# Hybrid decoder trunk: the first two weight groups of each feed-forward stage side by side, token parts split two at once

## The chip, the cores and the metric

The kernel runs on one core of one Trainium2 chip. The metric is the device time of the whole program in microseconds (us); lower is better.

## The reference

512 tokens of width 1024 pass through two layers. Each layer adds half a SwiGLU feed-forward (width 2816), then a mixer, then half of a second feed-forward; each of the three takes a root-mean-square norm of the running sum `h`. All in float32:

```
for layer in range(DEPTH):                       # DEPTH = 2
    h = h + 0.5 * _swiglu(_rmsnorm(h, norm_ffn1[layer]), ffn1_wg[layer], ffn1_wu[layer], ffn1_wd[layer])
    hn = _rmsnorm(h, norm_mix[layer])
    if layer % 2 == 0:
        h = h + _attn_conv_mixer(hn, ...)        # windowed attention | causal convolution, one output projection
    else:
        h = h + _recurrent_mixer(hn, ...)        # gated linear recurrence, output projection
    h = h + 0.5 * _swiglu(_rmsnorm(h, norm_ffn2[layer]), ffn2_wg[layer], ffn2_wu[layer], ffn2_wd[layer])
return _rmsnorm(h, norm_final)

def _swiglu(x, wg, wu, wd):
    return (jax.nn.silu(x @ wg) * (x @ wu)) @ wd
```

So there are four feed-forward stages, one even and one odd mixer, and a final norm.

## The kernel before, in words

**Products.** Tensors lie with the model width on the 128 partitions and the 512 tokens along the free axis. A float32 product is made of three matmuls of a rounded high half and a low rest: high by high, high by low, low by high. ScalarE (ACT) makes the high half (`hi`) by a copy to fp32r, VectorE (DVE) the low half (`lo`) by a subtraction. That holds for the weights (`raw` to `hi` and `lo`, tiles of 128 x 1024 or 128 x 768) and for the tokens (`split`, tiles named `t`).

**Seven products for eight.** The four feed-forward stages take the token axis and the inner axis in halves and use the seven-product form of a 2 x 2 block product. The products are called 1 to 7. Each wants one weight form, summed from four raw blocks, and one token part. `FORMS` says how a weight form is made: `q` holds block 0 (form 1); block 2, loaded into `r`, is added by DVE (form 7); block 3 and later block 1 are added to `q` by accumulating DMAs on GpSimd's (POOL's) queue (forms 6 and 3); block 3 is added to `r` the same way (form 5); forms 2 and 4 are plain loads on SyncE's (SP's) queue. The forms of one `q` are thus a chain. `Quarters` holds the token side: `make` builds one part (for 5, 7, 6 and 4 a difference first), then splits it into one tile, high half left, low half right.

**A stage.** The 22 chunks of the inner width are paired into 11 groups, in three rounds (`ROUNDS`) of 4, 4 and 3. Group 0 is multiplied the plain way (`two_by_chunk`, `project`) out of the unnormalized tokens and scaled afterwards by the norm factor `r`; its matmuls run while `r` is found (`inv_root`: a sum over partitions, then twelve small DVE operations). When `r` is there, the 28 token parts of the normed input (`xq`, four chunks by seven) are made, in the order 1, 2, 7, 5 and 6, 3, 4. The other groups take the seven products, 24 matmuls of 256 columns each. After each round two down groups (`downs`) take the round's results back to the model width, with 24 matmuls a product, 18 in the last round, and their products are added to `h` (`add_to`). `BANK` says which PSUM bank a product uses: 1, 6, 5 and 3 follow each other in `u`, 7 and 4 in `v`, 2 has `w`; a later product of a bank waits until the earlier sum has been read. `sequence` fixes the order of products: that of a group interleaves with the one before it.

**The order of instructions.** All operations are first recorded by `Plan.add` and then ordered for each engine by a list scheduler (`Plan.schedule`) with modelled costs; each operation has a due time, the matmul time recorded so far plus `plan.late`. An operation with a positive `late` is low: it may take a new `t` tile only when seven are free (`RESERVE`). Pools of numbered tiles limit how far things run ahead: `T_SLOTS` tiles `t` of 2 KB a partition, `RAWS` raw weights, `PARTS` high and as many low weight halves, of 4 KB each. `take` has weights recorded twelve units ahead (`AHEAD`), due 25 us early (`EARLY_PREP`), and the `hi` copies keep the order of the units. Since every instruction is emitted in `Plan.emit`, all of them carry line 426 in the profile; tiles tell them apart.

Of the kernel before, what the change touches and what calls it, by code (L numbers as in the profile page):

```python
# [64 lines left out]
T_SLOTS = 70  # L65
RAWS = 7
PARTS = 4
# [4 lines left out]
START_PREP = 9000.0  # L72
EARLY_LN = -40000.0
# [108 lines left out]
class Plan:  # L182
# [59 lines left out]
    def add(self, alts, late=None, after=None):  # L242
# [3 lines left out]
        for meth, a, k in alts[0][1]:  # L246
            for i, v in enumerate(a):
                if isinstance(v, _View):
                    (writes if i == 0 else reads).append(v.vt)
            for key, v in k.items():  # L250
                if isinstance(v, _View):
                    (writes if key in ("out", "accum_out") else reads).append(v.vt)
        op.alts = []
        op.table = None
        for eng, calls in alts:
            cs = [self.cost(eng, *c) for c in calls]
            op.alts.append((eng, sum(c for c, _ in cs), any(l for _, l in cs), calls))
# [12 lines left out]
        for t in reads:  # L270
            assert t.writers, t.name
            op.preds.update(t.writers[-1:])
# [157 lines left out]
def trunk(ctx, tc, A, out):  # L430
# [34 lines left out]
    class Group:  # L465


        def __init__(self, aps, chunks):
            self.aps, self.chunks = aps, chunks
            self.n = 2 * chunks * P  # L470
            self.raw, self.w, self.banks, self.open = {}, {}, {}, set()

    def sequence(groups, needs):


        out, last = [], None
        for g in groups:
            if last is None:
                out += [(g, "1", 0), (g, "2", 0), (g, "7", 0), (g, "6", 0)]
            elif needs(g, last):  # L480

                out += [(g, "1", 0), (last, "5", 0), (g, "7", 1), (last, "3", 0), (last, "4", 0)]
                out += [(g, "7", 2), (g, "6", 0), (g, "2", 0)]
            else:
                out += [(g, "1", 0), (last, "5", 0), (g, "2", 0), (g, "7", 0), (last, "3", 0), (last, "4", 0), (g, "6", 0)]
            last = g
        return out + [(last, m, 0) for m in ("5", "3", "4")]

    def ffn_units(w, l, final):
# [4 lines left out]
        for r, members in enumerate(ROUNDS):  # L494
# [4 lines left out]
            for d in DUALS[: 1 if final and r == len(ROUNDS) - 1 else 2]:  # L499
# [3 lines left out]
                order.append(downs[r, d])  # L503
        steps = sequence(order, lambda g, last: g in downs.values() and last in ffs.values())
# [64 lines left out]
    def prep_():  # L569
# [5 lines left out]
        else:  # L575
            n = src.n
            key, load, other, more = FORMS[what]
            for k, b in load.items():
# [3 lines left out]
            if other is not None:  # L582
                nc.vector.tensor_tensor(out=raw[:, :n], in0=raw[:, :n], in1=src.raw[other][:, :n], op=ALU.add)
            if more is not None:
                kw = dict(out=raw[:, :n], in_=src.aps[more], accum_op=ALU.add)
                plan.add([("SW", [("dma_start", (), kw)])])
        hi = plan.tile("hi", (P, WMAX), F32R)
# [56 lines left out]
    h = [pairs[j // 2][:, j % 2, :] for j in range(NJ)]  # L644
# [91 lines left out]
    def inv_root(parts, inv_n, eps, b0=0, nb=NB):  # L736
        pst = ps()
        for b in range(b0, b0 + nb):
# [6 lines left out]
        nc.vector.tensor_scalar(out=v[:], in0=pst[:, :nb], scalar1=inv_n, scalar2=eps, op0=ALU.mult, op1=ALU.add)  # L745
        nc.vector.tensor_scalar(out=sh[:], in0=v[:].bitcast(I32), scalar1=1, scalar2=None, op0=ALU.logical_shift_right)
        nc.vector.tensor_scalar(
            out=y[:].bitcast(I32), in0=sh[:], scalar1=-1, scalar2=0x5F3759DF, op0=ALU.mult, op1=ALU.add
        )
        for _ in range(3):  # L750
            nc.vector.tensor_tensor(out=w[:], in0=y[:], in1=y[:], op=ALU.mult)
            nc.vector.scalar_tensor_tensor(out=w[:], in0=w[:], scalar=-0.5, in1=v[:], op0=ALU.mult, op1=ALU.mult)
            nc.vector.scalar_tensor_tensor(out=y[:], in0=w[:], scalar=1.5, in1=y[:], op0=ALU.add, op1=ALU.mult)
# [38 lines left out]
    def scaled(o, r):  # L792
        t = tt()
        late, plan.late = plan.late, EARLY_EVICT
# [7 lines left out]
    class Quarters:  # L802
# [13 lines left out]
        def make(self, m):  # L816
# [9 lines left out]
            elif m == "4":  # L826
                ve.scalar_tensor_tensor(out=t[:, HI], in0=t[:, LO], in1=b[:, LO], **kw)
            src = {
# [5 lines left out]
            self.parts[m] = x[:, LO], x[:, HI]  # L834

# [26 lines left out]
    def ffn(which, gain, gain_next):  # L862
# [20 lines left out]
        for names in (("1",), ("2",), ("7",), ("5", "6"), ("3",), ("4",)):  # L883
            for j, q in enumerate(xq):
                for m in names:
                    if m == "1":
                        normed(q.a, j, LO)
                    elif m == "2":
# [614 lines left out]
```

## Time and profile before

| | |
|---|---|
| median of 3 runs | 1756.18 us (1755.38 to 1757.98) |
| profiled execution | 1756.76 us |
| its span, first to last instruction | 1755.0 us |
| mean granted clock of TensorE | 0.984 of 2.4 GHz |
| busy in the span | TensorE 1693.3, VectorE 1430.5, ScalarE 963.9, GpSimd 259.7 us |
| HBM read | 264.90 MB, 153 GB/s over the span |

The profile is of one execution. An engine's busy time is what its instructions cover; the time between is idle, and the profile names what released the instruction behind it. TensorE (PE) is near the whole span; what it doesn't cover lies in a few places, which the rows below single out. The four feed-forward stages run at about 0 to 355, 490 to 880, 880 to 1235 and 1400 to 1755 us, the even mixer between the first and the second, the odd one between the third and the fourth.

### The profile page before, as it was taken

The page shows a single profiled execution, that of the slowest core. Times are in us where ns is not written, and L with a number is a line of the kernel's source. Part 1 is how long each engine was busy: PE and PEld are TensorE (multiplying, and loading weights), DVE is VectorE, ACT ScalarE, POOL GpSimd, SP SyncE. Part 2 cuts the span into 40 slices and gives each one's busy share as a digit, 9 for nine tenths or more (in the row PEclk, how much of TensorE's full clock was granted, in tenths as well). Part 3 has the DMA queues.
Part 4 walks back from the last instruction along what each step waited for, and adds up shares of the span by engine and source line. Part 5 has one row for each costly group of instructions (what it writes and reads, how often), then busy time and mean ns, then how long its engine had stood idle before and what let it go on. Part 6 is the DMA issues. An engine that isn't in the chain of part 4 may idle for free. (4 is left out here: it accounts for less than half of the span.)

```text
span 1755.0 us, 31057 instructions
## 1 busy us (share of the span) xinstructions
PE 1693.3 (96%) x12294; PEld 1591.3 (91%) x12294; DVE 1430.5 (82%) x2382; ACT 963.9 (55%) x1611; POOL 259.7 (15%) x286
## 2 busy tenths in 40 slices
PE   8999999999899999999998999999999989999997
PEld 6899999978578899999978999999787889999997
DVE  7987877879957987877899878778788598778686
ACT  5755645554634654645556546455485366465465
POOL 0011111118502111111100111111011011111110
PEclk8999999999989999999999999999999999999999
DMA  6687777632013677777646677776332256776761
GB/s 222 147 239 192 183 179 194 151 117 89 32 68 89 146 185 188 187 176 194 153 127 158 180 182 192 179 192 153 107 120 84 84 133 169 178 197 170 198 151 49
DMA packets 78257, 269.02 MB, mean 153 GB/s; under 512 B 8688, under 2 KB 11040, under 8 KB 77984
## 3 DMA queue, kind: packets, MB, share of 16 engines
q0 software_dynamic: 27216, 96.35, 31.9%
q1 hardware_dynamic: 50896, 170.69, 26.9%
q8 instruction: 96, 1.57, 0.4%
q14 instruction: 49, 0.40, 0.1%
HBM read 264.90 MB, written 3.68 MB: 153 GB/s over the span
## 5 line engine op out<-in xcount | busy, mean ns | idle before, releaser
L426 PE MATMUL ps<-t,hi 128*128 128x256 f32 (+1 forms) x7948 | 1573.8, 298 | 29.5 <-ACT t L426 13.6
L426 PEld LDWEIGHTS ps<-t,hi 128*128 128x128 f32 x7948 | 1266.0, 190 | 85.9 <-ACT t L426 20.3
L426 PE MATMUL ps<-t,lo 128*128 128x256 f32 (+1 forms) x3974 | 1180.0, 297 | 8.4 <-DVE lo L426 8.2
L426 ACT ACTIVATE hi<-raw 128x1024 fp32r<-128x1024 f32 (+1 forms) x507 | 520.3, 1037 | 503.3 <-PE ps L426 218.5
L426 PEld LDWEIGHTS ps<-t,lo 128*128 128x128 f32 x3974 | 756.7, 190 | 33.5 <-DVE lo L426 11.2
L426 DVE TENSOR_TENSOR lo<-raw,hi 128x1024 fp32r<-128x1024 f32 (+1 forms) x498 | 590.4, 1195 | 181.7 <-ACT hi L426 179.2
L426 ACT ACTIVATE t<-t 128x256 fp32r<-128x256 f32 (+4 forms) x605 | 241.0, 428 | 199.9 <-DVE t L426 194.0
L426 DVE TENSOR_TENSOR t<-t,t 128x256 fp32r<-128x256 f32 (+3 forms) x592 | 257.4, 461 | 19.0 <-ACT t L426 17.1
L426 POOL DMA_DIRECT2D raw<-in_ffn_gu x120 | 104.9, 874 | 792.5 <-DVE lo L426 504.2
L426 DVE SCALAR_TENSOR_TENSOR h<-ps,h 128x512 f32<-128x512 f32 (+1 forms) x169 | 110.7, 671 | 21.5 <-PE ps L426 21.0
L426 ACT ACTIVATE t<-ps 128x512 f32<-128x512 f32 (+3 forms) x212 | 101.8, 490 | 41.3 <-PE ps L426 39.4
L426 POOL DMA_DIRECT2D raw<-in_ffn_down x69 | 60.3, 874 | 412.9 <-DVE lo L426 284.3
L426 DVE TENSOR_TENSOR t<-t 128x256 f32<-128x256 f32 x180 | 74.5, 417 | 7.5 <-ACT t L426 7.3
L426 DVE TENSOR_TENSOR t<-t,ps 128x512 f32<-128x512 f32 (+1 forms) x124 | 73.3, 594 | 7.1 <-ACT t L426 4.2
L426 DVE TENSOR_TENSOR raw<-raw,raw 128x1024 f32<-128x1024 f32 (+1 forms) x63 | 76.4, 1213 | 0.4
L426 DVE SCALAR_TENSOR_TENSOR t<-h,vec,t 128x256 f32<-128x256 f32 (+1 forms) x112 | 64.2, 601 | 6.6 <-ACT t L426 6.5
L426 POOL TENSOR_TENSOR t<-t,t 128x512 f32<-128x512 f32 (+1 forms) x42 | 56.8, 1372 | 56.1 <-ACT t L426 52.4
L426 DVE TENSOR_TENSOR t<-ps,t 128x512 f32<-128x512 f32 (+1 forms) x86 | 51.3, 611 | 10.0 <-PE ps L426 5.5
L426 DVE SCALAR_TENSOR_TENSOR ps<-raw,vec,ps 128x512 f32<-128x512 f32 x84 | 57.4, 746 | 2.2 <-POOL t L426 1.6
L426 DVE SCALAR_TENSOR_TENSOR t<-t,t 128x256 f32<-128x256 f32 (+1 forms) x128 | 54.5, 434 | 2.3 <-ACT t L426 1.0
L426 PE MATMUL ps<-t,t 128*128 128x512 f32 (+2 forms) x140 | 42.3, 455 | 9.1 <-ACT t L426 4.5
L426 ACT ACTIVATE t<-h,vec 128x512 fp32r<-128x512 f32 (+2 forms) x60 | 41.0, 686 | 9.9 <-DVE h L426 8.4
(61 smaller groups left out, 389.5 us busy)
## 6 DMA issues: line engine op xcount, KB each, us to landing
raw<-in_ffn_gu SPq DMA_DIRECT2D x160, 512.0 KB, 4.6
raw<-in_ffn_gu POOLq DMA_DIRECT2D x120, 512.0 KB, 5.3
raw<-in_ffn_down SPq DMA_DIRECT2D x64, 512.0 KB, 4.8
raw<-in_ffn_down POOLq DMA_DIRECT2D x48, 512.0 KB, 5.3
raw<-in_ffn_down SPq DMA_DIRECT2D x28, 384.0 KB, 3.6
raw<-in_odd_in SPq DMA_DIRECT2D x16, 512.0 KB, 4.2
raw<-in_ffn_down POOLq DMA_DIRECT2D x21, 384.0 KB, 4.8
raw<-in_ffn_first SPq DMA_DIRECT2D x14, 512.0 KB, 3.3
```

What stands on the lines that cost most here:

```text
L426: getattr(getattr(nc, _ENG[eng]), meth)(*(real(v) for v in a), **{q: real(v) for q, v in k.items()})
```

## The change

- `sequence`: the first two groups of a stage go through products 1, 2, 7, 6 and 5 side by side; their 3 and 4 come in among the third group's. The last group of a stage takes 7 and 6 ahead of 2, and the end is 5, 4, 3 in place of 5, 3, 4.
- Those two groups (`first`) take block 2 into `q` by an accumulating DMA, and load it again into `r` for form 5.
- Token parts are made by pairs, 2 and 3, 5 and 7, 6 and 4, each pair with one split of 512 columns (`make_two`).
- Group 0's evictions, its SwiGLU and parts get later due times, and weight sums and splits due times 10 or 15 us later than the loads'.
- Six `hi` and `lo` tiles for four, six raw tiles for seven, 64 `t` tiles for 70.
- The norm's twelve operations are planned as one, and `h` is eight planned tiles in place of four pairs.

```diff
-T_SLOTS = 70
-RAWS = 7
-PARTS = 4
+T_SLOTS = 64
+RAWS = 6
+PARTS = 6
+CHAIN_PART = 10000.0
+LONE_PART = 15000.0
+NEEDED = {"1": 0.0, "23": 5000.0, "57": 9000.0, "64": 17000.0}
+GROUP0_EVICT = 6000.0
+GROUP0_LATE = 40000.0
...
     def sequence(groups, needs):
-        out, last = [], None
-        for g in groups:
-            if last is None:
-                out += [(g, "1", 0), (g, "2", 0), (g, "7", 0), (g, "6", 0)]
+        g, last = groups[:2]
+        out = [(x, m, 0) for m in ("1", "2", "7", "6", "5") for x in (g, last)]
+        extra = [(g, "3", 0), (g, "4", 0)]
+        for g in groups[2:]:
+            if extra:
+                out += [(g, "1", 0), *extra, (last, "3", 0), (g, "2", 0), (g, "7", 0), (last, "4", 0), (g, "6", 0)]
+                extra = []
             elif needs(g, last):
...
+            elif g is groups[-1]:
+                out += [(g, "1", 0), (last, "5", 0), (g, "7", 0), (last, "3", 0), (last, "4", 0), (g, "6", 0), (g, "2", 0)]
             else:
                 out += [(g, "1", 0), (last, "5", 0), (g, "2", 0), (g, "7", 0), (last, "3", 0), (last, "4", 0), (g, "6", 0)]
             last = g
-        return out + [(last, m, 0) for m in ("5", "3", "4")]
+        return out + [(last, m, 0) for m in ("5", "4", "3")]
...
             key, load, other, more = FORMS[what]
+            if what == "7" and src.first:
+                load, other, more = {}, None, 2
+            elif what == "5" and src.first:
+                load = {"r": 2}
...
+                plan.late += CHAIN_PART
                 nc.vector.tensor_tensor(out=raw[:, :n], in0=raw[:, :n], in1=src.raw[other][:, :n], op=ALU.add)
+                plan.late -= CHAIN_PART
...
+        chain = kind == "form" and key == "q"
+        plan.late += CHAIN_PART if chain else LONE_PART
         hi = plan.tile("hi", (P, WMAX), F32R)
...
+        def make_two(self, m, n):
+            src = {"23": self.b, "57": self.s, "64": self.t}[m + n]
+            self.sums(m)
+            self.sums(n)
+            hi, lo = tt(F32R), tt(F32R)
+            split(src[:], hi[:], lo[:])
+            self.parts[m] = hi[:, LO], lo[:, LO]
+            self.parts[n] = hi[:, HI], lo[:, HI]
...
-        for names in (("1",), ("2",), ("7",), ("5", "6"), ("3",), ("4",)):
+        for names in ("1", "23", "57", "64"):
+            plan.late = NEEDED[names]
...
-            t1 = scaled(og, r)
-            t2 = scaled(ou, r)
+            t1 = scaled(og, r, False)
+            t2 = scaled(ou, r, False)
+            plan.late = GROUP0_LATE
             swiglu(x[:], (t1[:], t1[:]), t2[:])
-        for m in ("1", "2", "7", "5", "6", "3", "4"):
-            gq[0].make(m)
+            plan.late = 0.0
+        plan.late = GROUP0_LATE
+        gq[0].make("1")
+        for names in ("57", "23", "64"):
+            gq[0].make_two(*names)
+        plan.late = 0.0
...
-                for name in ("7", "5", "6"):
-                    q.make(name)
+                q.make_two("5", "7")
+                q.make("6")
...
-            if m == "4" and rnd == len(ROUNDS) - 1:
+            if m == ("3" if g is steps[-1][0] else "4") and rnd == len(ROUNDS) - 1:
```

## Rows read from the trace of the kernel before

**Rows 1.** The page, part 1: busy us of each engine, share of the span, instructions.

```profile
PE 1693.3 (96%) x12294; PEld 1591.3 (91%) x12294; DVE 1430.5 (82%) x2382; ACT 963.9 (55%) x1611; POOL 259.7 (15%) x286
```

**Rows 2.** The page, part 2: granted clock of PE, tenths, 40 slices.

```profile
PEclk8999999999989999999999999999999999999999
```

**Rows 3.** Stretches: us, busy PE, PEld, DVE, ACT, POOL (instructions), clock, DMA share, GB/s.

```profile
38.00:70.00 32.00, 26.33 (x184) 24.06 (x184) 32.00 (x72) 21.67 (x44) 2.60 (x3) 0.95 0.43 103
575.00:596.00 21.00, 17.50 (x129) 15.85 (x130) 21.00 (x45) 13.34 (x28) 2.62 (x3) 1.00 0.67 158
913.00:950.00 37.00, 30.64 (x222) 29.02 (x221) 36.01 (x78) 21.96 (x46) 3.49 (x4) 0.91 0.54 126
1421.00:1453.00 32.00, 26.12 (x193) 24.46 (x193) 31.28 (x64) 18.91 (x40) 4.38 (x5) 0.95 0.57 132
350.00:370.00 20.00, 16.64 (x97) 14.86 (x97) 18.70 (x26) 13.16 (x20) 0.40 (x1) 0.91 0.67 204
...
100.00:320.00 220.00, 220.00 (x1858) 220.00 (x1858) 175.04 (x252) 116.78 (x179) 29.42 (x34) 1.00 0.78 197
```

**Rows 4.** Waits of PE, 913 to 945 us: us in total, times, longest.

```profile
PE ps L426 <- DVE lo L426: 2.6, 3, 0.9
PE ps L426 <- ACT t L426: 2.1, 2, 1.4
```

**Rows 5.** Timeline of PE, third start: start, us, instruction [idle before and releaser].

```profile
913.45 0.40 PE L426 MATMUL ps<-t,hi 128*128 128x256 f32 x2
...
942.01 0.79 PE L426 MATMUL ps<-t,hi 128*128 128x256 f32 x2 [1.42 <-ACT t L426]
```

**Rows 6.** Timeline of DVE, third start; x is the number merged.

```profile
905.96 1.29 DVE L426 TENSOR_TENSOR t<-ps,t 128x512 f32<-128x512 f32 x2
907.16 1.27 DVE L426 SCALAR_TENSOR_TENSOR t<-h,vec,t 128x256 f32<-128x256 f32 x3
...
918.73 2.35 DVE L426 TENSOR_TENSOR lo<-raw,hi 128x1024 fp32r<-128x1024 f32 x2
...
934.70 1.76 DVE L426 TENSOR_TENSOR t<-t,t 128x256 fp32r<-128x256 f32 x5
```

**Rows 7.** Groups by form, DVE, 906 to 942 us: count, busy us, mean ns, idle.

```profile
L426 DVE TENSOR_TENSOR lo<-raw,hi 128x1024 fp32r<-128x1024 f32 x9 | 10.9, 1215 | 0.0
L426 DVE TENSOR_TENSOR t<-t,t 128x256 fp32r<-128x256 f32 x27 | 10.2, 416 | 0.0
L426 DVE SCALAR_TENSOR_TENSOR t<-h,vec,t 128x256 f32<-128x256 f32 x16 | 7.1, 477 | 0.0
...
L426 DVE TENSOR_TENSOR raw<-raw,raw 128x1024 f32<-128x1024 f32 x1 | 1.2, 1218 | 0.0
```

**Rows 8.** The chain that ended last, 1216 to 1240 us, end of the third stage.

```profile
1225.09 6.42 DMA raw<-in_ffn_down
```

**Rows 9.** Timeline of PE, end of the third stage.

```profile
1228.20 0.47 PE L426 MATMUL ps<-t,hi 128*128 128x256 f32 x2 [0.88 <-DVE h L426]
...
1232.51 0.50 PE L426 MATMUL ps<-t,hi 128*128 128x256 f32 x2 [1.94 <-ACT hi L426]
1233.50 0.58 PE L426 MATMUL ps<-t,lo 128*128 128x256 f32 x1 [0.49 <-DVE lo L426]
```

**Rows 10.** Groups by form, whole run.

```profile
L426 POOL DMA_DIRECT2D raw<-in_ffn_gu x120 | 104.9, 874 | 792.5 <-DVE lo L426 504.2 <-DVE raw L426 168.9 <-DVE t L426 112.7
...
L426 DVE TENSOR_TENSOR t<-t,t 128x512 fp32r<-128x512 f32 x16 | 11.2, 715 | 0.8 <-ACT t L426 0.7
```

**Rows 11.** Timeline of ACT, end of the third stage.

```profile
1209.43 0.85 ACT L426 ACTIVATE hi<-raw 128x768 fp32r<-128x768 f32 x1 [0.20 <-PE ps L426]
```

**Rows 12.** Waits, all engines, 100 to 320 us.

```profile
ACT hi L426 <- PE ps L426: 36.5, 26, 2.2
```

**Rows 13.** Waits of SP's DMA queue, 100 to 320 us.

```profile
SPq L426 <- DVE lo L426: 106.2, 30, 8.8
```

**Rows 14.** Groups by form, POOL, 906 to 945 us.

```profile
L426 POOL DMA_DIRECT2D raw<-in_ffn_gu x6 | 5.2, 872 | 62.6 <-DVE raw L426 33.3 <-DVE lo L426 29.3
```

## What was predicted

> **What bounds the kernel now.** I read the page first. TensorE (PE) is busy for 1693.3 of 1755.0 us [rows 1], so the change can win back only idle time of PE and time at the lower clock. In the 40 slices [rows 2] the granted clock reads 9 nearly everywhere, 8 in two of them; a slice of 44 us is too coarse for more. So I cut the span into shorter stretches [rows 3]. In mid-stage, 100 to 320 us, PE is busy for all of its 220 us at full clock; 1858 matmuls there make 118 ns each, so one of the seven products of a feed-forward group (24 matmuls) costs 2.8 us, and one of a three-chunk down group (18) costs 2.1 us. The loss sits at the four stage starts: 5.7, 3.5, 6.4 and 5.9 us idle, 21.4 us together, and the clock of 0.95, 1.00, 0.91 and 0.95 costs 1.6 + 0 + 3.3 + 1.6 = 6.5 us more. And it sits at the ends of the first three stages, of which the first is shown: 3.4 us idle and a clock of 0.91 over 20 us (1.8 us); the other two differ from it by 0.1 us, so 15.3 us in all. Starts and ends make 43 us; the full clock is 2.4 GHz, the lower one 1.2 GHz, and a mean of 0.91 is 18% of a stretch at the lower one.
>
> At the starts DVE is the cause. In the third one DVE has hardly an idle us and PE waits in turn for token parts (t) and for the low half of weights (lo) [rows 3, 4]. Projection ends and the first group's products begin at 913.5 us [rows 5], and the last wait ends at 942.0 us; the first token part could be begun only at 907.2 us, when the norm factor was there [rows 6]. What DVE does from 906 to 942 us is in [rows 7]: 27 subtractions of token parts, 28 being all of them, all 16 norm products, nine weight halves of 1.2 us, one raw add; the rest is evictions and the differences between parts.
>
> At the ends the cause is a chain of one raw weight tile. At the third, an accumulating DMA was issued at 1225.09, landed 6.42 us later, and ACT and DVE split what it brought before PE could go on [rows 8]: 1.94 and 0.49 us lost, after 0.88 us for an eviction of h between products 6 and 5, which share a bank [rows 9].
>
> **The change part by part.** The sum is made against the profiled execution, 1756.8 us, whose span is 1755.0; it stands 0.6 us above the median, 1756.2.
>
> *Starts: the cost on DVE.* Instructions in a row start 0.335 us apart at 256 columns (five in 1.76 us), about 0.60 at 512 (two in 1.29 us), weight halves 1.13 (two in 2.35 us), norm products of 256 columns 0.40 (three in 1.27 us), all in [rows 6]. Token parts of one chunk cost 4 norm products, 4 differences and 7 subtractions: 1.6 + 1.34 + 2.35 = 5.3 us, 21.2 us for four chunks. After the change: 2 norm products of 256 and one of 512 columns (0.67), 4 differences, one subtraction of 256 and three of 512: 0.8 + 0.67 + 1.34 + 0.34 + 1.8 = 4.95 us, 19.8 us for four. Only 1.4 us is saved. (By mean durations, 416 ns in [rows 7] against 715 ns in [rows 10], it would be 0.12 us for each of 16 merged pairs, 1.9 us; durations overlap in a queue, so I take the starts.) The Trainium skill, Perfetto Trace Analysis, section Optimizing Scalar/DVE Operations, gives about 60 ns of fixed cost for each DVE instruction on SBUF and says that the profiled latency is about twice that; 16 merged pairs would save 1.0 us by it, on the side of the starts. The same section says that breaking instructions up can let work finish sooner where the engine isn't saturated, which is an argument against pairing parts; here DVE is saturated.
>
> Other DVE relief inside that stretch: the first two groups take form 7 by an accumulating DMA in place of a raw add (one in the stretch: 1.1 us); the deferred second SwiGLU of group 0 (0.6 us; its parts came behind the last wait anyway, so deferring them gives little); two more part tiles let about two weight halves be made before the norm factor is there (2.3 us). 36 us of DVE work becomes about 36 - 1.4 - 1.1 - 0.6 - 2.3 = 30.6 us; the last token part comes at 936.6 in place of 942.
>
> *Starts: when PE wants it.* Side by side, six products (1, 2 and 7 of both groups) can run without the last pair of parts, 16.8 us of PE; product 6 wants its first chunk at 913.5 + 16.8 = 930.3 and its last at 932.4. 936.6 is 4.2 us late; before, the lag was 6.4 us. One product of the third group, whose bank is free, can fill 2.8 us of it if its weights are split by then. So 2.2 to 5.0 us of 6.4 come back. I take a little over half, over four starts 11 of 21.4 us, and 2 of the 6.5 us of clock, since gaps of the same kind remain: 13 us. Bounds: nothing (the earlier deadline eats the relief) and 27.9 us.
>
> *Ends.* Product 2 of the last group moves between 6 and 5, and 4 between 5 and 3. The 0.88 us for the eviction behind 6 is then covered by 2.1 us of product 2. Product 3 is wanted 2.1 us (2) and 2.1 us (4) later than before, against 2.4 us of lateness, and two more part tiles start the chain up to 4.2 us earlier, since the split that begins it waited for PE to free a tile [rows 11]. So this wait should go. New is a wait behind product 5: product 4 writes the bank that the second eviction of 5 reads, and both evictions add to the same h tile, one after the other: 0.88 + 0.60 = about 1.5 us. Per end 3.3 - 1.5 = 1.8 us come back, and of the clock's 1.8 us I take 1.2: 3.0 us, 9 us for three. Bounds: 0 and 15.3 us.
>
> *Costs elsewhere.* Eight more accumulating DMAs (one for each of two groups, four stages), one raw tile and six t tiles fewer, the same bytes in two more tiles of each part pool. In mid-stage the splits wait for PE to free part tiles, 26 times [rows 12], so their data is there early and a raw tile fewer has cover; SP does wait for raw tiles to come free (106 us over 220) [rows 13], and without the cover each late chain would cost the 2.4 us of an end. The even mixer keeps four raw tiles through its convolution, which leaves two in place of three for weights. I put 3 us; bounds 0 and 25 us (about ten late chains). The norm's twelve small operations planned as one, and h as single chunks, change the planner's order only: nothing, within 2 us either way.
>
> Sum: 1756.8 - 13 - 9 + 3 = 1737.8, against the median 1737.2; I say 1738.
>
> **The rivals.** (a) *The starts don't gain.* DVE's work shrinks by a seventh, but the parts are wanted earlier, 930 us against 936 us (before, the last part that PE waited for was wanted eight products, 22.4 us, behind 913.5); the lag stays at about 6 us and only the ends give: 1756 - 9 + 2 = 1749. For it speaks that PE already took ready products out of turn. (b) *Both losses close nearly whole.* 27.9 + 10 - 3 = 35 us: 1721. For it: the first waits are for weights (2.6 of 6.4 us in [rows 4]), which two more tiles feed. (c) *The raw pool becomes the bound.* With six raw tiles and two to four chains of accumulating DMAs a group, every round of a stage waits once for a chain as the ends do now: 12 rounds at 2.4 us are 29 us, less the 22 us above and with 2 us of clock lost: about 1765. It decides from nine such waits on. Against it: the mid-stage has none now. (d) *Slower DMA issue on POOL.* The eight moved loads wait behind DVE; POOL's six issues in the saturated stretch took 872 ns each, against 874 ns over the whole run [rows 10, 14], so a wait of, say, one weight half (1.2 us) each would be 10 us at most, 1747. The Trainium skill, SBUF — State Buffer, section SBUF: two separate sides, says that a DVE operation in a two-port mode keeps GpSimd from writing descriptors; the trace does not bear it out for these DVE operations. (e) *It cancels out*, or the plan turns out nearly as before: within 3 us of 1756.
>
> **How the numbers follow.** The forecast (1730 to 1745) 0.46; (a) 0.18; (b) 0.12; (c) 0.13; (d) 0.01; (e) 0.10. A change of 0.2% (3.5 us) is about what this measurement can tell. Faster: 0.46 + 0.18 + 0.12 + 0.01 = 0.77, same 0.10, slower 0.13. For the range I leave out the slow half of (c) and the fast half of (b): 1721 to 1759.
>
> **What would show it.** In the profile after: idle PE in the four starts about 10 us in place of 21, with waits for t where products 6 begin; at the ends one wait of 0.9 to 1.5 us behind DVE h and none behind ACT hi, and a clock near 1.00; eight raw adds of 1024 columns fewer; mid-stage still 220 of 220 us. I am wrong if mid-stage shows waits for lo or hi behind a DMA, if the starts still lose 20 us, or if the mixers between 380 and 560 or 1240 and 1400 us grow.

## The result and the profile after

The changed kernel takes 1715.76 us (median of 4 runs, 1714.08 to 1716.73) beside 1755.86 us for the kernel before on the same chip: a ratio of 0.9768, 95% interval 0.9751 to 0.9785. That is 40 us faster; 18 were forecast, and the time lies 5 us under the range. The profiled execution took 1715.53 us, its span 1713.5.

The page after, part 1 (busy us, share, instructions) and the clock row of part 2, to set against [rows 1, 2]:

```profile
PE 1674.6 (98%) x12294; PEld 1578.0 (92%) x12294; DVE 1410.0 (82%) x2257; ACT 956.6 (56%) x1515; POOL 267.9 (16%) x291
...
PEclk9999999999999999999999999999999999999999
```

PE has as many matmuls as before and is busy for 19 us less. Matmuls at the lower clock take longer and count as busy: in the kernel before three of 256 columns begin 0.64 us apart from 1233.9 to 1236.4 us, where the granted clock is 0.50, and 0.36 us apart behind that, at 1.00. The mean granted clock went from 0.984 to 0.991. By these means the clock cost 28 us of the span before and 15 after, an estimate, so most of the 19 us is clock won back. The stretches after, in the order of [rows 3] (four starts, then the ends of the first and the third stage, then mid-stage; busy PE, PEld, DVE, ACT, POOL with instructions, clock, DMA share, GB/s):

```profile
34.00:66.00 32.00, 25.98 (x179) 24.03 (x178) 30.23 (x55) 18.26 (x28) 2.98 (x4) 0.89 0.69 162
561.00:582.00 21.00, 19.79 (x162) 19.14 (x161) 21.00 (x36) 12.44 (x21) 2.62 (x3) 1.00 0.71 164
890.00:927.00 37.00, 32.71 (x249) 32.26 (x248) 36.77 (x65) 22.96 (x36) 3.52 (x4) 0.91 0.54 122
1388.00:1420.00 32.00, 29.37 (x224) 28.87 (x223) 28.82 (x49) 20.48 (x31) 3.40 (x4) 0.89 0.62 161
342.00:362.00 20.00, 20.00 (x141) 18.60 (x140) 19.21 (x26) 15.46 (x23) 0.00 (x0) 1.00 0.79 261
1188.00:1208.00 20.00, 20.00 (x163) 19.67 (x162) 17.92 (x24) 12.28 (x17) 0.88 (x1) 1.00 0.76 237
100.00:320.00 220.00, 219.54 (x1852) 219.28 (x1851) 175.29 (x250) 116.79 (x170) 29.42 (x34) 1.00 0.75 188
```

The two ends shown have neither idle time nor a lower clock left. The starts have both: 6.0, 1.2, 4.3 and 2.6 us idle, 14 in place of 21.4, and the clock of three of them reads 0.89 to 0.91. By the prediction's own reckoning that clock costs 3.5 + 0 + 3.3 + 3.5 = 10.3 us, more than the 6.5 before. Mid-stage is nearly full, as before.

**Loss by place.** To compare whole kernels I took from the records of PE, for each place, its time less what its weight products take at full rate. A matmul of 256 columns counts 0.118 us (220 us for 1858 of them in [rows 3]), one of 512 columns 0.233 us (15 in 3.49 us of the changed kernel's third projection, from 886.42 us on). The places are cut at the same shares of the product work in every kernel. The loss so holds idle time, the lower clock, and matmuls that are no weight products (attention, transposes, norms), which are the same in all kernels and make up much of the beginning and of the even mixer.

| us lost | beginning | four starts | three ends | even mixer | last stage's tail | rest | sum |
|---|---|---|---|---|---|---|---|
| before | 25.3 | 38.2 | 21.1 | 61.6 | 9.8 | 18.8 | 174.8 |
| after | 21.7 | 28.4 | 1.2 | 56.9 | 6.6 | 19.4 | 134.3 |
| difference | -3.6 | -9.8 | -19.9 | -4.6 | -3.2 | +0.6 | -40.5 |

### The profile page after: what moved, and what is told of

Read it like the earlier page. It is cut to its first block, busy times and chain, and to the rows that moved or that the text cites. A ratio compares the mean times of both kernels' runs of the same rounds, so it can differ in the third digit from the quotient of the medians.

```text
span 1713.5 us, 30831 instructions
## 1 busy us (share of the span) xinstructions
PE 1674.6 (98%) x12294; PEld 1578.0 (92%) x12294; DVE 1410.0 (82%) x2257; ACT 956.6 (56%) x1515; POOL 267.9 (16%) x291
## 4 chain that ended last, share of the span: by engine, by line
PE 81%; DVE 11%; DMA 3%; ACT 2%; issue 2%; POOL 0%; SPq 0%; ACTq 0%; POOLq 0%; DVEq 0%
PE ps L437 81%; DVE t L437 7%; DVE lo L437 3%; ACT t L437 2%; DMA raw<-in_ffn_gu 2%; DMA raw<-in_ffn_down 1%; ACT hi L437 1%; DVE ps L437 0%; DMA t<-in_ffn_first 0%; DVE raw L437 0%; DVE s L437 0%; DMA h<-in_x 0%; POOL t L437 0%; POOL lo L437 0%; SPq L437 0%
## 5 line engine op out<-in xcount | busy, mean ns | idle before, releaser
L437 PEld LDWEIGHTS ps<-t,hi 128*128 128x128 f32 x7948 | 1261.4, 190 | 70.1 <-DVE t L437 14.3
L437 ACT ACTIVATE t<-t 128x256 fp32r<-128x256 f32 (+3 forms) x505 | 225.4, 475 | 125.9 <-DVE t L437 119.5
L437 DVE TENSOR_TENSOR t<-t,t 128x256 fp32r<-128x256 f32 (+3 forms) x492 | 251.2, 530 | 7.2 <-ACT t L437 6.4
L437 POOL DMA_DIRECT2D raw<-in_ffn_gu x128 | 112.0, 894 | 809.0 <-DVE lo L437 529.4
L437 DVE SCALAR_TENSOR_TENSOR h<-ps,h 128x512 f32<-128x512 f32 (+1 forms) x169 | 113.4, 674 | 56.5 <-PE ps L437 55.7
L437 DVE SCALAR_TENSOR_TENSOR t<-h,vec,t 128x512 fp32r<-128x512 f32 (+2 forms) x96 | 61.9, 666 | 9.8 <-ACT t L437 9.7
L437 DVE TENSOR_TENSOR raw<-raw,raw 128x1024 f32<-128x1024 f32 (+1 forms) x55 | 65.0, 1182 | 1.4 <-DMA raw<-in_ffn_gu 1.4
L437 DVE SCALAR_TENSOR_TENSOR ps<-raw,vec,ps 128x512 f32<-128x512 f32 x84 | 57.5, 744 | 0.4 <-POOL t L437 0.4
L437 ACT ACTIVATE t<-h,vec 128x512 fp32r<-128x512 f32 (+2 forms) x60 | 40.5, 684 | 16.2 <-DVE h L437 16.2
```

What stands on the lines that cost most here:

```text
L437: getattr(getattr(nc, _ENG[eng]), meth)(*(real(v) for v in a), **{q: real(v) for q, v in k.items()})
```

## The experiments

In the labels, a_ is the changed kernel with something undone, b_ the kernel before with one part of the change. Ratios are to the kernel before on the same chip, with 95% intervals; the table at the end of this section has the loss by place of each run.

**The planner's noise.** The order of all instructions comes out of one list scheduler, so any edit shifts it everywhere. a_jitter changes one modelled cost by 5 ns and means nothing by it:

```diff
-_LAT = {"PE": 200.0, "ACT": 220.0, "DVE": 140.0, "POOL": 200.0, "SP": 2300.0, "SW": 4100.0}
+_LAT = {"PE": 205.0, "ACT": 220.0, "DVE": 140.0, "POOL": 200.0, "SP": 2300.0, "SW": 4100.0}
```

> The changed kernel with one modelled latency of the planner moved by 5 ns (a matmul's result, 205 for 200), which changes no instruction, only what the planner takes for due. Theory N (the even mixer's loss, 55 to 67 us in the runs so far, is the plan's chance and belongs to no part of the change): the losses in the starts and ends stay within 1.5 us each, the even mixer moves by several us, the time by up to 10 us either way. Rival (each loss is set by the order of the work): all within 2 us.

Measured: 1715.82 us, 0.9768 (0.975 to 0.9785). The total is the same, but a single start moves by up to 2 us, the four together by 4.4 and the rest by 4.5; the even mixer moves by 0.8 only, so this edit doesn't show its loss to be chance. Differences of a place below this are not read in what follows. It is one edit, and another may move more.

**The ends: order and pools.** The end order and the pools, each undone, and each by itself in the kernel before. a_end:

```diff
-            elif g is groups[-1]:
-                out += [(g, "1", 0), (last, "5", 0), (g, "7", 0), (last, "3", 0), (last, "4", 0), (g, "6", 0), (g, "2", 0)]
...
-        return out + [(last, m, 0) for m in ("5", "4", "3")]
+        return out + [(last, m, 0) for m in ("5", "3", "4")]
...
-            if m == ("3" if g is steps[-1][0] else "4") and rnd == len(ROUNDS) - 1:
+            if m == "4" and rnd == len(ROUNDS) - 1:
```

> The changed kernel with the old order at the stage ends (last group 1, 5 of the one before, 2, 7, ...; end 5, 3, 4). Theory A (the order closes the ends): the ends lose 2 to 5 us each again, 6 to 15 us in all, about 1725. Rival B (six part tiles for four start the chain of raw sums early enough by themselves): the ends stay shut but for the 0.9 us behind products 6 and 5, so at most 3 us, 1716 to 1719.

a_pools sets `T_SLOTS`, `RAWS`, `PARTS` from 64, 6, 6 back to 70, 7, 4:

> The changed kernel with the old pools (70 t tiles, 7 raw, 4 high and low halves). Rival B (the deeper part pools do nearly all): 25 us or more come back, 1741 and up. Theory A: the stage ends lose again what two products of earlier preparation gave, about 2 us each, and the starts a few us; 6 to 14 us, 1722 to 1730.

a_end_pools does both. b_end is the kernel before with the diff of a_end the other way round, b_pools with the new pools, b_end_pools with both:

> The changed kernel with the old order at the ends and the old pools, so with the changes at the starts, the single h tiles and the joined norm alone. Theory A (parts add up by place): the beginning at 21.5, the starts at about 27, the ends back at 6 to 7 each, about 1738. Rival (the starts need the deeper part pools): the starts above 33 us, 1745 and up.

> The kernel before with two things of the change alone: the order at the stage ends and the pool sizes. Theory A (these two close the ends): the three ends lose under 1 us each in place of 6.3 to 6.7, the starts stay as before, about 1737 to 1740. If the wait that the prediction put behind product 5 (1.5 us, with part of the clock's loss) were real, the ends would still lose 2 to 3 us each: 1743 to 1747.

> The kernel before with the pools of the change alone: 64 tiles t, six raw tiles, six part tiles of each kind. Theory (pools and end order each close part of an end: about 7.0 us lost with neither, 4.8 with the new pools alone, 2.1 with the new order alone, under 1 with both): the three ends lose 4.5 to 5.2 us each, so 6 to 7 us come back there, and the total is 1746 to 1752. Rival (the six part tiles are what closes the ends, the order adds little): ends of 1 to 2 us, total under 1742. Rival of the prediction's cost term (a raw tile fewer costs): mid-stages lose more than 3 us each and the total is 1756 or above.

> The kernel before with the order of the last two groups' products alone (7 and 6 ahead of 2; 5, 4, 3 at the end). Theory: the ends lose 1.9 to 2.4 us each, with a wait of 0.9 to 1.5 us behind DVE's eviction h and no product of the next stage in it, so 14 to 15 us come back and the total is 1741 to 1745. By the prediction's sum, which takes 1.8 us of waits and 1.2 us of clock an end: 1747. Rival (the order without the six part tiles still waits for the last raw chain): ends of 4 us or more, total above 1747.

| | in the changed kernel: us, loss of the three ends | in the kernel before: us, loss of the three ends |
|---|---|---|
| old order, old pools | 1740.92 (a_end_pools), 21.0 | 1755.86, 21.1 |
| old order, new pools | 1741.82 (a_end), 14.3 | 1737.86 (b_pools), 13.7 |
| new order, old pools | 1732.76 (a_pools), 6.3 | 1757.81 (b_end), 17.5 |
| new order, new pools | 1715.76, 1.2 | 1734.45 (b_end_pools), 2.8 |

Ratios: a_end 0.9926 (0.9906 to 0.9945), a_pools 0.9871 (0.9854 to 0.9888), a_end_pools 0.9905 (0.9889 to 0.992), b_pools 0.9908 (0.9893 to 0.9923), b_end 1.0022 (1.0009 to 1.0035), b_end_pools 0.9869 (0.985 to 0.9887).

The totals missed what was expected of a_end and a_pools (1716 to 1725; 1722 to 1730, or 1741 and more), because the even mixer loses 10 and 9 us more there; by place the ends came out near the first theory of each. a_end_pools and b_end_pools came out within 3 us of theirs; b_end closes far less than expected.

Only both together close the ends, in either kernel. What each alone leaves is in the rows of the third end. The new order with the old pools, a_pools, PE and then ACT:

```profile
1221.35 0.48 PE L437 MATMUL ps<-t,hi 128*128 128x256 f32 x2 [1.29 <-DVE h L437]
...
1220.03 1.06 ACT L437 ACTIVATE hi<-raw 128x1024 fp32r<-128x1024 f32 x1 [0.42 <-ACT hi L437]
```

The old order with the new pools, a_end, PE and then DVE:

```profile
1224.22 0.77 PE L437 MATMUL ps<-t,hi 128*128 128x256 f32 x2 [2.76 <-DVE h L437]
...
1222.51 0.96 DVE L437 TENSOR_TENSOR lo<-raw,hi 128x768 fp32r<-128x768 f32 x1 [0.52 <-ACT hi L437]
1223.39 0.68 DVE L437 SCALAR_TENSOR_TENSOR h<-ps,h 128x512 f32<-128x512 f32 x1
```

The changed kernel at the same place, PE and then ACT:

```profile
1201.54 0.40 PE L437 MATMUL ps<-t,hi 128*128 128x256 f32 x2
1201.77 0.28 PE L437 MATMUL ps<-t,lo 128*128 128x256 f32 x1
1201.89 0.63 PE L437 MATMUL ps<-t,hi 128*128 128x512 f32 x2
1202.37 0.39 PE L437 MATMUL ps<-t,lo 128*128 128x512 f32 x1
1202.60 0.63 PE L437 MATMUL ps<-t,hi 128*128 128x512 f32 x2
1203.07 0.40 PE L437 MATMUL ps<-t,lo 128*128 128x512 f32 x1
1203.30 0.40 PE L437 MATMUL ps<-t,hi 128*128 128x256 f32 x2
...
1198.32 1.04 ACT L437 ACTIVATE hi<-raw 128x1024 fp32r<-128x1024 f32 x1
```

In a_pools the 1.29 us are the wait for an eviction of h that the prediction foresaw behind product 5; the stage's last two products, 36 matmuls, follow it. In the changed kernel six matmuls of 512 columns stand there, from 1201.89 to 1203.30: the first chunk of the projection that comes next, here the odd mixer's, with its first two weights. ACT made the high half of the first from 1198.32 us on, 3.6 us ahead of its use; in a_pools it begins that at 1220.03, as PE's pause begins. The six matmuls take 1.41 us, and no wait follows them. The other two ends have the same six, at 350.29 and 861.83 us. The three pool sizes were changed together, so that the two more part tiles do this, and not the other two sizes, is argued and not shown. In a_end PE waits ahead of product 5, as before [rows 9], and for longer: on DVE the eviction stands behind a weight's low half, for which DVE itself waited for ACT.

b_end, the new order with the old pools in the kernel before:

```profile
1219.88 0.51 PE L426 MATMUL ps<-t,hi 128*128 128x256 f32 x2 [0.85 <-DVE h L426]
...
1223.16 0.48 PE L426 MATMUL ps<-t,hi 128*128 128x256 f32 x2 [0.88 <-DVE h L426]
...
1235.33 0.50 PE L426 MATMUL ps<-t,lo 128*128 128x512 f32 x1 [0.67 <-DVE lo L426]
```

From 1223.16 PE runs 90 matmuls of 256 columns without a pause, five products of 18: by the order of instructions 3 and 4 of the group before the last, then 6, 2 and 5 of the last. So the eviction behind 6 is covered here, and behind 5 PE takes up the projection, with 0.67 us of waiting in it. The two waits of 0.85 and 0.88 us stand ahead of 5 and 3 of the group before the last; from between these two the new order took product 2 away. They are a cost of the order that no sum had. b_end brought 3.6 us at the three ends and not the 14 to 15 expected of it; of the 3.6 us an end that are missing, these two waits make 1.7. The same step brings 14.7 in the changed kernel (a_end_pools against a_pools), where these two waits are missing; why they are isn't settled. The later due times of weight sums and splits are one of several differences between the two kernels, and no run takes them back.

The clock at these ends, in the columns of [rows 3]: a_pools, b_end, a_end.

```profile
1216.00:1236.00 20.00, 18.71 (x120) 16.76 (x119) 18.68 (x28) 11.22 (x17) 0.00 (x0) 1.00 0.62 208
1215.00:1235.00 20.00, 17.72 (x140) 16.66 (x139) 17.90 (x26) 13.29 (x19) 1.75 (x2) 1.00 0.80 218
1216.00:1236.00 20.00, 17.24 (x118) 16.15 (x117) 17.46 (x23) 14.63 (x21) 0.00 (x0) 0.91 0.71 207
```

So the new order by itself has the full clock at this end, even with waits left.

The pools alone are worth 16 us in the kernel before (b_pools), and 7.4 come back at the ends, as expected. At the starts they bring about 8 us and not the 15 that the table below seems to show. PE's first wait for a token part lies on the border of two places there; b_pools and b_end_pools both have it:

```profile
43.80 0.58 PE L426 MATMUL ps<-t,hi 128*128 128x256 f32 x1 [4.78 <-ACT t L426]
43.89 0.58 PE L426 MATMUL ps<-t,hi 128*128 128x256 f32 x1 [4.93 <-ACT t L426]
```

The table counts it to the beginning in b_pools and to the starts in b_end_pools. Counted as in b_end_pools, b_pools loses about 26 us in the beginning and 30 in the starts, and nearly all that it gains in the starts it gains in the fourth.

**The starts: order, pairs, group 0.** a_seq takes the first two groups one after the other again, form 7 by DVE:

```diff
-        g, last = groups[:2]
-        out = [(x, m, 0) for m in ("1", "2", "7", "6", "5") for x in (g, last)]
...
+        out, last = [], None
+        for g in groups:
+            if last is None:
+                out += [(g, "1", 0), (g, "2", 0), (g, "7", 0), (g, "6", 0)]
...
-            g.first = True
+            g.first = False
```

> The changed kernel with the old order at the stage starts (one group after the other, form 7 by a DVE add, nothing else undone). Theory A (side by side is worth little, since DVE bounds the starts either way: the starts lose about 25 us in both traces): within 5 us of 1715.8. Rival C (side by side is what the starts gained, and without it paired parts come too late): the four starts lose 10 to 20 us more, 1726 to 1736.

Measured: 1724.15 us, 0.9823 (0.9805 to 0.9841); the starts lose 35.5 us in place of 28.4. Side by side is worth about 7 us there, between the two expectations; PE's waits for weights in the four starts are 4.8 us in place of 1.4.

a_two makes each part with a split of its own:

```diff
-            hi, lo = tt(F32R), tt(F32R)
-            split(src[:], hi[:], lo[:])
...
+            self.make(m)
+            self.make(n)
```

> The changed kernel with every token part split by itself again (the pairs' order kept, two splits of 256 columns for one of 512, in the starts and in all later groups). By the prediction's term the pairing saved DVE about 0.3 us a pair of four chunks, 1 to 1.5 us a start: 4 to 6 us in all, about 1721. Rival: pairing delays the first part of a pair and is worth nothing in the starts, within 2 us of 1715.8 or faster.

Measured: 1716.42 us, 0.9768 (0.9747 to 0.9789). Pairing brings nothing that can be measured; at the starts alone the single splits are no worse (21.6 us lost against 28.4), and other places give that back. The Trainium skill, Perfetto Trace Analysis, section Optimizing Scalar/DVE Operations, says that grouping can help where an engine is saturated; DVE is so at the starts (36.77 of 37 us in the third), and these two runs don't bear it out for the twelve pairs of splits a start. The norm products that the change joins, four a start, stay joined in a_two.

a_group0 takes back group 0's later due times; a_needed0 those of the pairs; a_needed0_group0 both; b_group0 is the kernel before with group 0's later due times alone:

```diff
-NEEDED = {"1": 0.0, "23": 5000.0, "57": 9000.0, "64": 17000.0}
-GROUP0_EVICT = 6000.0
-GROUP0_LATE = 40000.0
+NEEDED = {"1": 0.0, "23": 0.0, "57": 0.0, "64": 0.0}
+GROUP0_EVICT = -40000.0
+GROUP0_LATE = 0.0
```

> The changed kernel with group 0's evictions, SwiGLU and parts due at once again. By the prediction deferring them gives little (they came behind the last wait before): within 3 us of 1715.8, the starts' losses unchanged. Rival: with six products unlocked at once their 5 us of DVE work now stands in the way of the pairs 57 and 64, so that the starts lose 3 to 5 us more each, 1727 to 1735.

> The changed kernel with all token parts due at once, group 0 still deferred. Theory D: the order of the pairs stays the same, so the starts change by under 2 us each, 1712 to 1722. Rival: the later due times leave room for evictions and weights in front of the pairs, and without them the starts lose 3 us more each, 1726 and up.

> The changed kernel with group 0 due at once and all token parts due at once as well (due times of the pairs 0 in place of 0, 5, 9, 17 us). Theory D (group 0's work hurts only because the change gave the pairs due times behind it; by the prediction it came last anyway when the parts were due first): the starts fall back from 56 us, with group 0 at once, to 25 to 35 us and the time from 1751 to about 1720 to 1728. Rival E (group 0's five us of VectorE work have to leave the start whatever the due times): the starts stay above 45 us, 1740 or more.

> The kernel before with the deferral of group 0 alone (evictions due 6 us, SwiGLU and parts 40 us later). By the prediction deferring gives little, since this work came behind the last wait: the starts' 38 us change by under 4 us, 1753 to 1757. Rival E: the deferral alone takes 10 us or more from the starts, 1747 or less.

| | us | ratio | four starts |
|---|---|---|---|
| a_group0 | 1751.15 | 0.9965 (0.9952 to 0.9978) | 56.5 |
| a_needed0 | 1717.7 | 0.9775 (0.9759 to 0.9792) | 27.1 |
| a_needed0_group0 | 1725.81 | 0.9822 (0.9805 to 0.9838) | 28.6 |
| b_group0 | 1759.16 | 1.0013 (1.0002 to 1.0023) | 28.4 |

The wait for a token part at the first start of a_group0, from PE's timeline:

```profile
72.53 0.58 PE L437 MATMUL ps<-t,hi 128*128 128x256 f32 x1 [5.34 <-ACT t L437]
```

Group 0's own parts then stand ahead of the pairs, which are due later, and the pairs come late: 28 us, far more than either expectation. With the pairs due at once that is gone, as theory D said (a_needed0_group0 loses 7 us more than a_needed0 in the even mixer, not in the starts). So most of what the deferral saves is a loss that the pairs' due times would bring. In the kernel before it takes 9.8 us out of the starts all the same, which its total hides (below).

**The norm and h.** a_root plans the norm's twelve operations one by one again; a_pairs plans h as four pairs again; b_h is the kernel before with h as eight tiles.

> The changed kernel with the norm's twelve small DVE operations planned one by one, as in the kernel before. By the prediction (an order of the plan only): within 2 us, 1714 to 1718. Rival (planned one by one, other DVE work gets in between them at the saturated starts, and each start waits longer for the norm factor): the four starts lose 4 us or more beyond the changed kernel's 28, total 1719 or above.

> The changed kernel with h planned as four pairs again. Theory A (each part of the change works at its own place; the single h tiles let the first loads and norms of the program start sooner): the beginning, up to the first product of the first feed-forward group, goes from 34.4 us back to about 39, the stage ends get a little of their wait back, and the time rises by 5 to 10 us, to about 1723. Rival B (the deeper part pools do nearly all): within 2 us of 1715.8.

> The kernel before with h as eight planned tiles in place of four pairs, and nothing else. Theory (single tiles of h let the first loads of x be issued ahead of the weights', and the first norm begin earlier): the beginning loses 21 to 22 us in place of 25.3 and the total is 1750 to 1754. By the prediction (an order of the plan only, nothing within 2 us): beginning as before, 1754 to 1758. Rival (the beginning gains, and the rearranged plan gives it back in the even mixer, whose loss was 55 to 72 us in the kernels so far): beginning 21 to 22 us, total 1754 to 1760.

Measured: a_root 1716.02 us, 0.9784 (0.9766 to 0.9803), nothing. a_pairs 1716.71, 0.9777 (0.9757 to 0.9798): the beginning loses 25.8 us again, and other places give it back. b_h 1771.1, 1.0096 (1.0079 to 1.0114): the beginning loses 21.1, as in the changed kernel, but the even mixer 77.2. The total of b_h lies far above all three expectations. Of the beginning's 4 us one wait of PE makes 3.5. Loads of x on SP's queue, that wait, and ACT's first work on x, first in the kernel before, then after:

```profile
11.07 0.43 SPq L426 DMA_DIRECT2D h<-in_x  x1
14.47 0.33 SPq L426 DMA_DIRECT2D h<-in_x  x1
...
9.62 1.58 PE L426 MATMUL ps<-t,t 128*128 128x512 f32 x2 [4.53 <-ACT t L426]
...
8.86 0.71 ACT L426 ACTIVATE t<-h,vec 128x512 fp32r<-128x512 f32 x1
```

```profile
8.30 1.79 SPq L437 DMA_DIRECT2D h<-in_x  x2
...
8.48 0.50 PE L437 MATMUL ps<-t,t 128*128 128x512 f32 x1 [1.00 <-ACT t L437]
...
3.46 0.63 ACT L437 ACTIVATE t<-h 128x512 f32<-128x512 f32 x1 [1.44 <-DMA h<-in_x]
```

As a pair is one planned tile, its norm work is ordered behind the load of both chunks; as single tiles the loads are all issued by 10.1 us in place of 14.8, and ACT begins on the first chunk at 3.46 us in place of 8.86.

**The even mixer's swing.** In the runs so far its loss went from 55 to 77 us. The timeline of ACT in b_h, just ahead of PE's longest wait, and that wait:

```profile
498.79 1.28 ACT L430 ACT_TABLE_LOAD   x1
500.09 1.52 ACT L430 ACTIVATE t<-t,vec 128x512 f32<-128x512 f32 x2
501.51 1.13 ACT L430 ACTIVATE t<-t 128x512 fp32r<-128x512 f32 x2
...
502.55 1.50 ACT L430 ACTIVATE t<-t,vec 128x512 f32<-128x512 f32 x2
503.96 1.13 ACT L430 ACTIVATE t<-t 128x512 fp32r<-128x512 f32 x2
...
505.11 1.28 ACT L430 ACT_TABLE_LOAD   x1
506.40 0.51 ACT L430 ACTIVATE t<-t,s 128x256 f32<-128x256 f32 x1
...
508.01 1.75 PE L430 MATMUL ps<-ident,t 128*128 128x128 f32 x7 [10.84 <-ACT t L430]
```

Between two exponentials of the last softmax ACT takes the four SiLU activations of the convolution and their splits, and loads its function table twice, 1.28 us each. b_group0 has the same, with a wait of 10.62 us; in a_end and a_pools, which lose 67 and 66 us there, PE waits 5.1 and 5.5 us behind the splits that follow those activations. b_h_silu orders those activations behind the last exponential:

```diff
+        begun = len(plan.ops)
         attention(q, k, v, sbias, acat_h, acat_l)
+        exps = [i for i in range(begun, len(plan.ops)) if plan.ops[i].table == {"exp"}]
...
-            nc.scalar.activation(cv[c][:], cv[c][:], AF.Silu, bias=col("ln_b", c), scale=col("ln_g", c))
+            kw = dict(bias=col("ln_b", c), scale=col("ln_g", c))
+            i = plan.add([("ACT", [("activation", (cv[c][:], cv[c][:], AF.Silu), kw)])])
+            plan.ops[i].preds.update(exps)
```

> The kernel before with h as eight planned tiles (b_h: 1771, even mixer 77 us lost), and the four SiLU activations of the convolution made to wait for the last exponential of the attention, so that ACT loads its function tables once between them and not twice. Theory (the two table loads and eight activations in the middle of the last softmax, 498.8 to 506.4 us in b_h, are what makes PE wait 10.8 us at 508): that wait goes, the even mixer loses 60 to 66 us, the total is 1754 to 1761, and the beginning still loses 21 to 22 us. Rival (the wait is the attention's own chain, the table loads lie in its shade): 1768 to 1773, the even mixer still above 73 us.

Measured: 1764.39 us, 1.0044 (1.0029 to 1.0059). One table load is left, PE's wait at that place is 3.9 us, and the even mixer loses 67.8 us in place of 77.2. The direction is the theory's, the size is not: 9.4 of the 15.6 us over the kernel before are gone, 6 remain, and the first start loses 4.3 us more than there. What sets those wasn't found. The same step for b_group0 wasn't tried: the run meant for it (b_group0_silu) took b_group0 itself once more, 1758.12 us, every place within 1.7 us of the first.

Loss by place of all runs, us:

| | beginning | four starts | three ends | even mixer | tail | rest | sum |
|---|---|---|---|---|---|---|---|
| a_jitter | 21.7 | 24.0 | 0.8 | 57.7 | 6.6 | 23.9 | 134.8 |
| a_end | 21.4 | 23.4 | 14.3 | 66.9 | 8.2 | 24.3 | 158.6 |
| a_pools | 20.9 | 29.4 | 6.3 | 65.8 | 7.9 | 22.8 | 153.1 |
| a_end_pools | 22.6 | 27.7 | 21.0 | 56.7 | 8.8 | 23.7 | 160.4 |
| b_end | 26.4 | 38.7 | 17.5 | 63.4 | 10.6 | 21.1 | 177.5 |
| b_pools (see above) | 32.9 | 23.0 | 13.7 | 57.5 | 8.1 | 22.7 | 157.7 |
| b_end_pools | 26.2 | 33.2 | 2.8 | 59.1 | 8.7 | 25.3 | 155.3 |
| a_seq | 21.4 | 35.5 | 1.8 | 59.8 | 6.5 | 19.8 | 144.8 |
| a_two | 22.5 | 21.6 | 2.2 | 58.3 | 7.4 | 24.9 | 136.9 |
| a_group0 | 21.8 | 56.5 | 1.7 | 64.9 | 6.6 | 22.5 | 174.2 |
| a_needed0 | 21.2 | 27.1 | 1.3 | 57.1 | 6.6 | 23.8 | 137.1 |
| a_needed0_group0 | 21.6 | 28.6 | 2.7 | 64.0 | 6.7 | 20.8 | 144.4 |
| b_group0 | 26.3 | 28.4 | 22.6 | 72.0 | 9.8 | 21.1 | 180.3 |
| a_root | 21.5 | 28.3 | 1.5 | 57.2 | 7.3 | 18.7 | 134.4 |
| a_pairs | 25.8 | 25.9 | 1.3 | 55.3 | 5.4 | 19.0 | 132.6 |
| b_h | 21.1 | 40.7 | 23.4 | 77.2 | 10.3 | 19.2 | 191.9 |
| b_h_silu | 21.2 | 41.9 | 22.0 | 67.8 | 9.8 | 20.0 | 182.8 |

## Why the prediction was wrong

The sign was right, the sum was not: -13 - 9 + 3 was forecast, and the places show -9.8 - 19.9 - 10.8. Of the 21.5 us that the sum fell short, the ends make 10.9 and the costs elsewhere 13.8; the starts gained 3.2 less than forecast.

**The step that failed: the ends.** "New is a wait behind product 5", 1.5 us, and a clock of which 1.2 of 1.8 us come back, made 3.0 us an end; 6.6 were measured. The wait is real: with the old pools it is there (1.29 us in a_pools). But it costs nothing in the changed kernel, since PE has the next projection to run in it. I asked what would be late next on PE's list for this stage and not what else PE could take up. That six part tiles let the next weights be split early stood in the prediction as a relief of the chain alone. The clock gives back its whole 1.8 us, where I had held back a third; the order alone has it at 1.00 at the third end, with waits left (a_pools, b_end). "The 0.88 us for the eviction behind 6 is then covered by 2.1 us of product 2" was right, in b_end too; that the new order leaves two evictions of the group before uncovered (0.85 and 0.88 us in b_end) stood in no term. They don't show in the changed kernel.

**The second step, and the larger in size: costs elsewhere.** 3 us of cost were forecast; 10.8 us came back. "h as single chunks, change the planner's order only: nothing, within 2 us" holds for the total in the changed kernel, where pairs cost 1 us (a_pairs), but not in the kernel before, which single tiles make 15 us slower (b_h). By place they are 4 us of the beginning in both. The norm as one operation is nothing, as said (a_root). The raw tile given up shows no cost either: PE is busy for 219.54 of 220 us in the first stage's middle, and in stretches of the second and third, 620 to 850 and 945 to 1180 us, for all of them. The even mixer's 4.6 and the tail's 3.2 us belong to no one part, and their cause stays open. The even mixer's loss hangs on where the plan happens to put the convolution's activations, which b_h_silu shows for 9.4 of 15.6 us of one case; that its 4.6 us were luck in the changed kernel is only argued.

**The starts: near in size, wrong in reasons.** 13 us were forecast, 9.8 measured, DVE is still without a pause (36.77 of 37 us in the third start) and 28 us are still lost. The prediction had the gain come from an earlier last token part, with 2 us of clock. PE's waits in the four starts (30 to 38 us of each), from the kernel before to after, say otherwise: those for token parts went from 14.0 to 12.8 us, those for weights (hi, lo) from 7.2 to 1.4, and the clock got no better (0.95, 1.00, 0.91, 0.95 to 0.89, 1.00, 0.91, 0.89). So the nearness of 9.8 to 13 is luck. PE's waits at the third start after, against [rows 4, 5]:

```profile
902.47 0.39 PE L437 MATMUL ps<-t,hi 128*128 128x256 f32 x1 [0.78 <-ACT t L437]
906.37 0.58 PE L437 MATMUL ps<-t,hi 128*128 128x256 f32 x1 [3.51 <-DVE t L437]
```

The forecast lag was 4.2 us, and 0.78 + 3.51 = 4.3 are seen, but not "where products 6 begin", so that too is luck: PE had done four products since 890.1, 96 matmuls, so it waits for parts of the pair 5 and 7 already in the products 7. What DVE did ahead of that pair's split:

```profile
900.96 2.35 DVE L437 TENSOR_TENSOR lo<-raw,hi 128x1024 fp32r<-128x1024 f32 x2
...
903.56 1.22 DVE L437 TENSOR_TENSOR lo<-raw,hi 128x1024 fp32r<-128x1024 f32 x1
...
905.63 1.28 DVE L437 TENSOR_TENSOR t<-t,t 128x512 fp32r<-128x512 f32 x2
```

Three weight halves stand ahead of the split that PE waits for, and they take nearly as long as the wait. It isn't the pairing: a_two has 3.31 us at this place, behind three halves as well, and the 1.4 us a start for pairing aren't seen. Whether the split ahead of those halves would be faster wasn't tried. "Deferring them gives little" was wrong in the kernel before, where the deferral by itself takes the starts from 38.2 to 28.4 us. The pools by themselves bring about 8 us there, near the 2.3 us a start put down for them, but mostly in the fourth start. All the parts together come to the same 28. The gains don't add; that each relieves the same engine until something else is late is argued, not shown.

**The rivals.** (b), both losses closing nearly whole, had the ends right; its 1721 was the nearest figure, and it had 0.12. Its reason, two more tiles that feed the waits for weights, doesn't hold: with the new pools alone these waits in the four starts are 7.6 us (b_pools) against 7.2, and the changed kernel with the old pools has none (a_pools). (a) falls, since the starts did gain. (c) falls: the middles of the stages have next to no wait. (e) falls with the 40 us. (d): POOL's 128 issues of these loads took 894 ns on average, against 874 for 120 before [rows 10], which is nothing:

```profile
L437 POOL DMA_DIRECT2D raw<-in_ffn_gu x128 | 112.0, 894 | 809.0 <-DVE lo L437 529.4 <-DVE raw L437 135.8 <-DVE t L437 47.8
```

The eight raw adds of 1024 columns are gone, as foreseen; before, then after:

```profile
L426 DVE TENSOR_TENSOR raw<-raw,raw 128x1024 f32<-128x1024 f32 x56 | 69.7, 1245 | 0.3
...
L437 DVE TENSOR_TENSOR raw<-raw,raw 128x1024 f32<-128x1024 f32 x48 | 58.4, 1216 | 1.4 <-DMA raw<-in_ffn_gu 1.4
```

## What to carry to other kernels

Where a wait is foreseen, ask what the waiting engine could run in its place, and what that work lacks; the new pools turned a wait of 1.3 us at a stage's end into useful matmuls of the next one. A product moved to cover one eviction may uncover another, so go through every eviction that it stood behind. An edit that changes the order alone should be costed at what the order may change, above all where planned units are joined or parted and where due times pass one another (28 us here between a deferral with and without its counterpart). In a kernel whose order comes from a scheduler, one part alone can look worthless because the plan pays for it somewhere else: compare by place and beside a meaningless edit before believing a total, and see that the border between two places doesn't cut through a wait.

## What was not expected of the hardware

A load of ACT's function table shows as a row of 1.28 us. Two of them, with the work between them, in the middle of a softmax go with a wait of PE of 10.8 us (b_h), and of 10.6 us in another kernel (b_group0); with one load behind the softmax the wait is 3.9 us (b_h_silu).
